# Mixture of eight experts on one core: the x of experts 0 and 1 as two halves of one tile

## The chip, the cores and the metric

The kernel runs on 1 core of one Trainium2 chip. The metric is device time in microseconds (us) of one execution; the time of a kernel is the median of several executions. A core has five engines that run side by side: TensorE (PE; its weight loads are shown as PEld), VectorE (DVE), ScalarE (ACT), GpSimd (POOL) and SyncE (SP). Transfers between the chip's main memory (HBM) and the core's memory (SBUF, 128 partitions) run on 16 DMA engines. POOL, SP and ACT can issue transfers, each into a queue of its own: in the profile q0 holds what POOL issues, q1 what SP issues, q10 what ACT issues.

## The reference

Each of 8 experts has 256 tokens of 512 numbers and two layers; all inputs are fp32.

```python
n_experts, capacity, hidden, expert_hidden = 8, 256, 512, 2048
# x [8,256,512]  w1 [8,512,2048]  w2 [8,2048,512]  b1 [8,2048]  b2 [8,512]
h = np.matmul(x, w1) + b1[:, np.newaxis, :]
h = np.maximum(h, 0)
return (np.matmul(h, w2) + b2[:, np.newaxis, :]).astype(np.float32)
```

One expert has 4.2 MB of w1 and as much of w2, so the weights are 67 MB in all; x and the result are 4.2 MB each.

## The kernel before, in words

All products are made in fp16 with fp32 sums. POOL's transfers turn fp32 in HBM into fp16 in SBUF on the way; SP's and ACT's move bytes as they are.

*Staging.* `w1_sb[e]` is a tile of 128 partitions, each with 4 rows of w1 (16 KB in fp16), `w2_sb[e]` one with 16 rows of w2 for each partition. Both come from pools of three buffers, so the load for expert e waits until the products of expert e-3 have read that buffer. The loads stand in `ring` (lines 260 to 270), an order with a stage for each: within a stage x (where `X_LOADS` has it), then w1, then w2 of the expert three behind. POOL issues them in that order (`ordered` keeps a queue's instructions in the order of the program).

*x and its turning.* The first product needs x with its 512 numbers along the partitions, so x has to be turned. There are three ways:
- Experts 4 to 7: one load by POOL (`load_x`, line 80), turned by DVE in 32x32 blocks (`turn_on_vector`, line 118).
- Experts 2 and 3: one load by POOL into one tile. Each expert has 64 partitions, each with R = 4 tokens. PE turns both experts together (`turn_on_tensor(2, 2)`, line 103): for two of the four rows at a time, 8 transposes of 128x128 into the PSUM tile `pt`, of which there is one buffer, and one copy on DVE (line 114, an "eviction") into `turned`. The columns of a turned block are then 64 tokens of one expert and 64 of the other, so an expert's x is 4 runs of 64 columns.
- Experts 0 and 1: SP loads each as fp32 into a tile of its own, with 128 partitions of R = 2 tokens, 4 KB (lines 224 to 227). DVE casts each to fp16 (line 247), and PE turns each by itself with `turn_on_tensor(e, 1)`: 8 transposes, one eviction.

PE's transposes need the unit matrix `ident`, which POOL, DVE and ACT make at the start (lines 236 to 243). DVE's order at the start is: `steps_turned` (line 240), then for each of experts 0 and 1 the cast and the eviction, then four transposes that lay out b1 as `b1T` (line 253), which wait for b1's own small load, `b_rows`.

*The products.* `first_product(e)` has 16 groups of 4 matmuls into a PSUM tile `ph` (three buffers); after each group ACT adds b1, applies the relu and writes `hT` (`relu`, line 130). The relu puts the tokens in the order that the store wants, by two forms of its access pattern that depend on R = `x16[e][2]`. Three stages later `second_product(e)` adds b2 and multiplies with w2 into `po`, and `store` copies `po` to an fp32 tile in SBUF.

*Results.* Experts 0 to 3 share one result tile (tag `out0`), experts 4 and 5 another (tag `out4`, 128 partitions of 8 KB, `group_pool`); POOL stores both at the end (`flush`). Experts 6 and 7 each have a tile of the pool `out_pool`, tag `out`, with two buffers, and are stored by SP and ACT. The two fp32 tiles for the x of experts 0 and 1 are the first two users of those buffers.

*The order of products* is the loop at line 272: in stage s the first product of expert s, then the second product of expert s-3.

Of the kernel before, what the change touches and what calls it, by code (L numbers as in the profile page):

```python
# [10 lines left out]
def kernel(  # L11
# [9 lines left out]
    nc = tc.nc  # L21
    fp32 = mybir.dt.float32
    fp16 = mybir.dt.float16
    E, T, H = x.shape
    M = w1.shape[2]
    P = 128
    nTB = T // P
# [8 lines left out]
    GROUPS = {0: 4, 4: 2}  # L36
# [5 lines left out]
    nXF32 = 2  # L42
# [3 lines left out]
    def ordered(ins):  # L46
        return tc.keep_in_program_order(ins)
# [4 lines left out]
    x_pool = ctx.enter_context(tc.tile_pool(name="xp", bufs=1))  # L52
# [3 lines left out]
    group_pool = ctx.enter_context(tc.tile_pool(name="groups", bufs=1))  # L56
    out_pool = ctx.enter_context(tc.tile_pool(name="outp", bufs=2))
# [13 lines left out]
    x16 = [None] * E  # L71
# [18 lines left out]
    def load_w1(e):  # L90
        w1_sb[e] = w1_pool.tile([P, nKC, M], fp16, tag="w1", name="w1sb")
        ordered(nc.gpsimd.dma_start(  # L92
            out=w1_sb[e], in_=w1[e].rearrange("(p kc) m -> p kc m", kc=nKC)
        ))
# [8 lines left out]
    def turn_on_tensor(first, n):  # L103

        t, _, R = x16[first]
        turned = turned_pool.tile([P, nKC, R, P], fp16, tag=f"turned{first}", name=f"turned{first}")
        for lo in range(0, R, nTB):
            pt = psum_x.tile([P, nKC, nTB, P], fp16, tag="pt", name="pt")
            for r in range(nTB):
                rows = t[:, lo + r, :].rearrange("p (i kc) -> p kc i", kc=nKC)  # L110
                for kc in range(nKC):
                    ordered(nc.tensor.transpose(  # L112
                        out=pt[:, kc, r, :], in_=rows[:, kc, :], identity=ident))
            ordered(nc.vector.tensor_copy(out=turned[:, :, lo : lo + nTB, :], in_=pt))  # L114
        for i in range(n):
            xT[first + i] = turned[:, :, :, i * (P // n) : (i + 1) * (P // n)]
# [104 lines left out]
                    ))  # L221
        store(e, po)

    x32 = []
    for e in range(nXF32):
        x32.append(out_pool.tile([P, nTB, H], fp32, tag="out", name="x32"))
        nc.sync.dma_start(out=x32[e], in_=x[e].rearrange("(p tb) h -> p tb h", tb=nTB))
    load_w1(0)
    ordered(nc.gpsimd.dma_start(  # L229
        out=b2_sb,  # L230
        in_=b2.rearrange("e h -> (e h)").rearrange("(o f) -> o f", o=1),
# [9 lines left out]
    for b in range(nB):  # L241
        part = slice(b * B, (b + 1) * B)
        nc.scalar.copy(out=ident[part, part], in_=steps_turned[part, :, 0])  # L243

    for e in range(nXF32):
        t = x_pool.tile([P, nTB, H], fp16, tag=f"x{e}", name=f"x{e}")
        ordered(nc.vector.tensor_copy(out=t, in_=x32[e]))  # L247
        x16[e] = (t, 0, nTB)
        turn_on_tensor(e, 1)


    for b in range(nB):
        ordered(nc.vector.transpose(  # L253
            out=b1T[b * B : (b + 1) * B, nB - 1 - b : nB - 1 - b + nJ * B],
            in_=b1_rows.rearrange("r (i j) -> r j i", j=nJ),
# [55 lines left out]
```

## Time and profile before

| | us |
|---|---|
| median of 3 executions | 181.64 |
| lowest and highest | 181.51, 182.15 |
| the profiled execution, its own time | 181.3 |
| its span in the trace | 179.5 |
| PE busy with matmuls | 133.4 |
| DVE busy | 42.9 |
| ACT busy | 72.6 |
| POOL busy | 14.9 |

The span is the time from the first to the last event of the core in the trace; the 1.8 us between it and the execution's time lie around it. Times inside the trace are counted from the start of the span. In the page's list of the span in 40 slices each digit is the busy share of a slice, in tenths. In a group of instructions, "x8" is how many there were, "128x1024 f16<-128x1024 f32" the shape and type of what is written and read, and what stands behind "<-" in brackets or behind a bar is the idle time of the engine just before and what ended it. The trace moved 40.55 MB of written bytes through the DMA engines, and read 71.39 MB of HBM.

### The profile page before, as it was taken

To read this page: it belongs to the slowest core of one execution; us is meant where nothing else is said; L and a number is where in the kernel's file an instruction comes from. 1 tells how busy PE (TensorE), PEld (TensorE's weight loads), DVE (VectorE), ACT (ScalarE), POOL (GpSimd) and SP (SyncE) were. 2 spreads that over 40 slices of the span, in tenths; PEclk is the share of its full clock that TensorE was granted. 3 is DMA by queue.
4 is the path that set the end of the run, shared out by engine and by line. 5 is a ranking of instruction groups with operands and counts; after the bars stand their busy time and mean duration, and the time that the engine had idled before them with its cause. 6 is when DMAs were issued, how large, how long until landed. Compare 5 with 4: busy or idle time off the path is not lost.

```text
span 179.5 us, 1952 instructions
## 1 busy us (share of the span) xinstructions
PE 133.4 (74%) x816; PEld 89.7 (50%) x816; DVE 42.9 (24%) x47; ACT 72.6 (40%) x157; POOL 14.9 (8%) x33
## 2 busy tenths in 40 slices
PE   0226499969499930999869994959798899999660
PEld 0114389969387410793358543933387343343220
DVE  0615400020000199409700691000600030301010
ACT  2200379939367250491167406940298002011010
POOL 7300003010201010001100001000100002002000
PEclk9999999999979996599987999987999699999998
DMA  5999999998998999999899999989999999999995
GB/s 207 260 223 203 234 204 204 234 230 179 236 230 184 228 234 208 201 234 226 190 226 234 204 204 234 223 186 234 226 194 223 234 204 203 212 218 219 329 434 248
DMA packets 3827, 40.55 MB, mean 226 GB/s; under 512 B 460, under 2 KB 476, under 8 KB 1260
## 3 DMA queue, kind: packets, MB, share of 16 engines
q0 software_dynamic: 3232, 38.35, 96.5%
q1 hardware_dynamic: 476, 1.70, 2.5%
q10 hardware_dynamic: 112, 0.39, 0.6%
q8 instruction: 6, 0.10, 0.2%
q14 instruction: 1, 0.01, 0.0%
HBM read 71.39 MB, written 4.19 MB: 421 GB/s over the span
## 4 chain that ended last, share of the span: by engine, by line
DMA 55%; PE 33%; another core or an unknown queue 3%; POOL 3%; ACT 2%; issue 1%; POOLq 0%
DMA w1sb<-in_w_dram 44%; PE ph L158 16%; PE po L215 16%; DMA w2sb<-in_w_dram 11%; ACT out L194 2%; PE po L208 1%; POOL w1sb L92 1%; POOL steps L236 1%; POOL x L84 0%; POOL w2sb L101 0%; POOL b_sb L229 0%; POOL b_rows L233 0%; ACT hT L145 0%; POOL steps L237 0%
## 5 line engine op out<-in xcount | busy, mean ns | idle before, releaser
L158 PEld LDWEIGHTS <-w1sb 128*128 128x128 f16 x512 | 60.6, 148 | 31.8 <-DMA w1sb<-in_w_dram 25.0
L145 ACT ACTIVATE hT<-ph,b1T 128x256 f16<-128x256 f32 x128 | 56.4, 474 | 33.3 <-PE ph L158 19.7
L215 PE MATMUL po<-w2sb,hT 128*128 128x512 f16 x256 | 59.9, 394 | 6.0 <-DMA w2sb<-in_w_dram 6.0
L215 PEld LDWEIGHTS <-hT 128*128 128x128 f16 x256 | 25.7, 101 | 40.1 <-issue 13.8
L158 PE MATMUL ph<-xT,w1sb 128*128 128x256 f16 x256 | 32.5, 293 | 14.1 <-DMA w1sb<-in_w_dram 13.9
L158 PE MATMUL ph<-turned,w1sb 128*128 128x256 f16 x256 | 33.7, 300 | 10.9 <-DMA w1sb<-in_w_dram 8.5
L194 ACT COPY out<-po 32x512 f32<-32x512 f32 (+2 forms) x22 | 12.7, 579 | 59.8 <-PE po L215 59.7
L124 DVE STREAM_TRANSPOSE xT<-x 32x1024 f16<-32x1024 f16 x16 | 19.8, 1236 | 43.5 <-DMA x<-in_x_dram 24.5
L193 DVE COPY out<-po 32x512 f32<-32x512 f32 (+2 forms) x20 | 13.8, 689 | 57.2 <-PE po L215 56.9
L101 POOL DMA_DIRECT2D w2sb<-in_w_dram x10 | 5.3, 534 | 72.3 <-PE po L215 72.3
L92 POOL DMA_DIRECT2D w1sb<-in_w_dram x8 | 4.8, 594 | 63.8 <-PE ph L158 63.0
L112 PE MATMUL pt<-ident,x 128*128 128x128 f16 x32 | 3.3, 263 | 8.8 <-ACT ident L243 6.7
L114 DVE COPY turned<-pt 128x1024 f16<-128x1024 f16 x4 | 2.8, 692 | 19.5 <-PE pt L112 19.5
L112 PEld LDWEIGHTS <-x 128*128 128x128 f16 x32 | 2.6, 126 | 9.2 <-DVE x L247 8.3
L253 DVE STREAM_TRANSPOSE b1T<-b_rows 32x512 f32<-32x512 f32 x4 | 4.1, 1034 | 4.8 <-DMA b_rows<-in_b_dram 4.8
L208 PE MATMUL po<-b_sb,ones 1*128 1x512 f16 x16 | 4.8, 379 | 0.0
L193 ACT COPY out<-po 32x512 f32<-32x512 f32 x2 | 1.2, 576 | 3.9 <-PE po L215 3.9
L243 ACT COPY ident<-steps_turned 32x32 f16<-32x32 f16 x4 | 1.0, 242 | 3.5 <-DVE steps_turned L240 3.5
L240 DVE STREAM_TRANSPOSE steps_turned<-steps 128x1024 f16<-128x1024 f16 x1 | 1.2, 1246 | 4.2 <-POOL steps L237 4.2
L208 PEld LDWEIGHTS <-ones 1*128 1x128 f16 x16 | 0.9, 92 | 2.1 <-issue 2.1
L243 ACT ACT_TABLE_LOAD x1 | 1.3, 1283 | 0.7 <-PEq L295 0.7
L247 DVE CAST x<-x 128x1024 f16<-128x1024 f32 x2 | 1.3, 667 | 0.0
(13 smaller groups left out, 5.5 us busy)
## 6 DMA issues: line engine op xcount, KB each, us to landing
w1sb<-in_w_dram POOLq DMA_DIRECT2D x8, 2048.0 KB, 34.5
w2sb<-in_w_dram POOLq DMA_DIRECT2D x6, 2048.0 KB, 48.2
w2sb<-in_w_dram POOLq DMA_DIRECT2D x2, 1024.0 KB, 27.2
out_dram<-out POOLq DMA_DIRECT2D x1, 2048.0 KB, 12.7
w2sb<-in_w_dram POOLq DMA_DIRECT2D x1, 1152.0 KB, 19.8
x<-in_x_dram SPq DMA_DIRECT2D x2, 512.0 KB, 3.7
x<-in_x_dram POOLq DMA_DIRECT2D x1, 1024.0 KB, 32.6
out_dram<-out POOLq DMA_DIRECT2D x1, 1024.0 KB, 8.3
```

The lines of the kernel that those rows point to most:

```text
L92: ordered(nc.gpsimd.dma_start(out=w1_sb[e], in_=w1[e].rearrange("(p kc) m -> p kc m", kc=nKC)))
L101: ordered(nc.gpsimd.dma_start(out=w2_sb[e][:, lo:hi], in_=src[:, lo:hi]))
L112: ordered(nc.tensor.transpose(out=pt[:, kc, r, :], in_=rows[:, kc, :], identity=ident))
L114: ordered(nc.vector.tensor_copy(out=turned[:, :, lo : lo + nTB, :], in_=pt))
L124: nc.vector.transpose(out=turned[b * B : (b + 1) * B], in_=src.rearrange("p r (i kc) -> p kc r i", kc=nKC),)
L145: nc.scalar.activation(out=out, in_=columns, func=mybir.ActivationFunctionType.Relu, bias=b1T[:, bias_at : bias_at + 1], scale=1.0,)
L158: ordered(nc.tensor.matmul(out=ph, lhsT=w1_sb[e][:, kc, :].rearrange("p (q j) -> p q j", j=nJ)[:, :, j], rhs=xT[e][:, kc], start=(kc == 0) ...
L193: on(out=out_sb[at : at + rows, k, :], in_=po[0][part])
L194: nc.scalar.copy(out=out_sb[at : at + rows, split + k, :], in_=po[1][part])
L208: ordered(nc.tensor.matmul(out=t, lhsT=ones1, rhs=b2_sb[0:1, e * H : (e + 1) * H], start=True, stop=False,))
L215: ordered(nc.tensor.matmul(out=po[tb], lhsT=hT[e][:, j, tb * P : (tb + 1) * P], rhs=w2_sb[e][:, j, :], start=False, stop=(j == nJ - 1),))
L253: ordered(nc.vector.transpose(out=b1T[b * B : (b + 1) * B, nB - 1 - b : nB - 1 - b + nJ * B], in_=b1_rows.rearrange("r (i j) -> r j i", j=nJ),
```

## The change

The fp32 x of experts 0 and 1 goes into one tile of 128 partitions with 4 tokens each (8 KB). Expert 0 has partitions 0 to 63, expert 1 partitions 64 to 127. SP still issues two loads of 512 KB, each as 64 rows of 8 KB into its half. DVE casts each half by itself, 64 partitions of 2,048 numbers. PE then turns both together with `turn_on_tensor(0, 2)`, as for experts 2 and 3. Since R is now 4 for these two experts, their first products read 4 runs of 64 columns and their relu uses the access pattern of experts 2 and 3. The number of transposes (16), of evictions (2) and of all other instructions is the same. The fp32 tile takes the room of the result tile of experts 4 and 5 (tag `out4`), and the buffers of `out_pool` belong to experts 6 and 7 alone.

The order on the engines: DVE has both casts, then both evictions, where it had cast, eviction, cast, eviction. PE's 16 transposes all read the common tile. POOL's order is the same.

```diff
-    x32 = []
+    R0 = nXF32 * T // P
+    x32 = group_pool.tile([P, R0, H], fp32, tag=f"out{max(GROUPS)}", name="x32")
+    of_expert = [slice(e * (P // nXF32), (e + 1) * (P // nXF32)) for e in range(nXF32)]
     for e in range(nXF32):
-        x32.append(out_pool.tile([P, nTB, H], fp32, tag="out", name="x32"))
-        nc.sync.dma_start(out=x32[e], in_=x[e].rearrange("(p tb) h -> p tb h", tb=nTB))
+        nc.sync.dma_start(out=x32[of_expert[e]], in_=x[e].rearrange("(p r) h -> p r h", r=R0))
     load_w1(0)
...
+    t = x_pool.tile([P, R0, H], fp16, tag="x0", name="x0")
     for e in range(nXF32):
-        t = x_pool.tile([P, nTB, H], fp16, tag=f"x{e}", name=f"x{e}")
-        ordered(nc.vector.tensor_copy(out=t, in_=x32[e]))
-        x16[e] = (t, 0, nTB)
-        turn_on_tensor(e, 1)
+        ordered(nc.vector.tensor_copy(out=t[of_expert[e]], in_=x32[of_expert[e]]))
+        x16[e] = (t, e * (P // nXF32), R0)
+    turn_on_tensor(0, nXF32)
```

## The prediction

> **What bounds the kernel now.** I read the page first: the slices over time, then the queues, then the chain that ended last.
>
> ```profile
> span 179.5 us, 1952 instructions
> ...
> PE 133.4 (74%) x816; PEld 89.7 (50%) x816; DVE 42.9 (24%) x47; ACT 72.6 (40%) x157; POOL 14.9 (8%) x33
> ...
> DMA  5999999998998999999899999989999999999995
> ...
> q0 software_dynamic: 3232, 38.35, 96.5%
> q1 hardware_dynamic: 476, 1.70, 2.5%
> ...
> DMA 55%; PE 33%; another core or an unknown queue 3%; POOL 3%; ACT 2%; issue 1%; POOLq 0%
> ```
>
> From the second slice to the last but one the DMA engines are full, while PE is busy 74% of the span. Queue q0 alone, which carries all the weights, takes 96.5% of the time of 16 engines. The busy times in stages say the same; the columns used here are the stretch and, at the end of each row, the DMA share and the GB/s.
>
> ```profile
> core 0: us, PE busy (x) PEld busy (x) DVE busy (x) ACT busy (x) POOL busy (x), PEclk, DMA share, GB/s
> 1.80:2.50 0.70, 0.00 (x0) 0.00 (x0) 0.00 (x0) 0.23 (x1) 0.70 (x3) 1.00 0.75 181
> 2.50:4.50 2.00, 0.00 (x0) 0.00 (x0) 0.26 (x1) 0.00 (x0) 2.00 (x6) 1.00 0.98 401
> ...
> 5.40:14.60 9.20, 2.06 (x16) 1.55 (x16) 2.65 (x5) 0.97 (x4) 0.78 (x1) 1.00 0.95 203
> 30.00:120.00 90.00, 70.92 (x489) 53.78 (x488) 28.03 (x28) 49.39 (x108) 4.97 (x10) 0.92 1.01 216
> ...
> 168.00:178.00 10.00, 4.04 (x18) 1.66 (x17) 0.69 (x1) 0.59 (x1) 0.00 (x0) 1.00 0.97 404
> ```
>
> The share is about 1.0 in every stage. Written bytes run at 216 GB/s where fp32 weights become fp16 on the way, and at 401 to 404 where fp32 stays fp32 (x at the start, the results at the end). So the kernel is one stream of transfers. The chain in order of time shows how far that stream's issues run ahead:
>
> ```profile
> 5.33 32.66 DMA w1sb<-in_w_dram
> ...
> 149.49 19.77 DMA w2sb<-in_w_dram
> ```
>
> w1 of expert 2 is issued by 5.33 and lands at 38.0; the last w2 piece is issued by 149.5 and lands at 169.3. The engines always have a backlog of ten microseconds or more. What makes the stream itself longer therefore moves the end one for one; what makes a compute engine later moves it only beyond the backlog.
>
> **The change part by part.**
>
> *The two loads of x.* Still two SP issues of 512 KB; each now fills 64 partitions with 8 KB, in place of 128 partitions with 4 KB. The DMA view of three stretches shows when x (q1) moves, and that w1 (q0) follows it.
>
> ```profile
> q1 hardware_dynamic: 34, 0.14, 26.2%
> ...
> q1 hardware_dynamic: 212, 0.80, 98.4%
> ...
> q1 hardware_dynamic: 288, 1.05, 53.5%
> q0 software_dynamic: 16, 0.26, 23.4%
> ```
>
> The first row is 0 to 2.5 us, the second 2.5 to 4.5, the last two 0 to 5.4. After a start of 0.14 MB, x fills the engines alone (98.4% in the second row); of w1 only 16 packets, one for each engine, begin before 5.4. While x moves, all 128 partitions together take 401 GB/s, 3.1 GB/s each. The end of the kernel, 404 GB/s, is no faster. No stretch in which the engines are full shows a partition at more than about that. The changed loads give the same engines half as many partitions at a time; to keep pace each would have to take 6.3 GB/s.
>
> No row shows a saturated load to 64 partitions, so I bound it. Below: nothing but packet size, half as many packets for the same bytes. Even if x moved at the best 426 GB/s that a half-microsecond of the load shows,
>
> ```profile
> 4.00:4.50 0.50, 1.00 1.03 426
> ```
>
> the remaining 1.05 - 0.14 = 0.91 MB would take 2.14 us for 0.91/0.401 = 2.27, a gain of 0.13. Above: a partition takes no more than now, the rate halves to 200 GB/s, and 0.91 MB takes 4.54 us, a loss of 2.27; with the start slowed alike it is 1.05/0.401 = 2.62. Between them lies 216 GB/s, the rate of writing while the weights stream, which gives 0.91/0.216 = 4.21, a loss of 1.94. I take +2.1, the middle of 1.94 and 2.27, because both rows of fp32 traffic (401 and 404) sit at the same rate per partition, and keep -0.13 and +2.62 as ends.
>
> The Trainium skill, SBUF — State Buffer, section "Door 1: The DMA port swizzle", speaks against the change: 64 adjacent partitions reach 8 of 16 ports, and it gives 196 GB/s for 1 MiB to partitions 0 to 63 against 328 to all 128; its section "Can I just issue two DMAs to hit both halves?" gives only 6% more for a pair at partitions 0 and 64. An estimate from that page is 1.05/0.208 - 1.05/0.328 = 1.85 us more; this trace holds no run that tests it.
>
> *The casts and the turning by PE.* The work around x as it stands:
>
> ```profile
> 4.24 1.25 DVE L240 STREAM_TRANSPOSE steps_turned<-steps 128x1024 f16<-128x1024 f16 x1 [4.24 <-POOL steps L237]
> ...
> 5.33 0.86 POOL L92 DMA_DIRECT2D w1sb<-in_w_dram  x1
> 5.41 0.65 DVE L247 CAST x<-x 128x1024 f16<-128x1024 f32 x1
> ...
> 6.67 1.01 PE L112 MATMUL pt<-ident,x 128*128 128x128 f16 x8 [6.67 <-ACT ident L243]
> 7.72 0.69 DVE L114 COPY turned<-pt 128x1024 f16<-128x1024 f16 x1 [1.66 <-PE pt L112]
> 8.33 0.68 DVE L247 CAST x<-x 128x1024 f16<-128x1024 f32 x1
> ...
> 9.07 1.04 PE L112 MATMUL pt<-ident,x 128*128 128x128 f16 x8 [1.38 <-DVE x L247]
> 10.15 0.69 DVE L114 COPY turned<-pt 128x1024 f16<-128x1024 f16 x1 [1.14 <-PE pt L112]
> ...
> 15.26 2.79 PE L158 MATMUL ph<-turned,w1sb 128*128 128x256 f16 x12 [5.15 <-DMA w1sb<-in_w_dram]
> 15.63 4.17 DVE L253 STREAM_TRANSPOSE b1T<-b_rows 32x512 f32<-32x512 f32 x4 [4.79 <-DMA b_rows<-in_b_dram]
> ...
> 28.61 0.53 POOL L92 DMA_DIRECT2D w1sb<-in_w_dram  x1 [22.43 <-PE ph L158]
> ```
>
> Each cast now has half the partitions and twice the columns: 0.67 us (unchanged) if its time goes by elements, 1.33 if by columns. The groups of copies of 512 columns on the same engine decide:
>
> ```profile
> L193 DVE COPY out<-po 32x512 f32<-32x512 f32 x14 | 9.6, 688 | 17.7 <-PE po L215 17.5
> ...
> L193 DVE COPY out<-po 128x512 f32<-128x512 f32 x2 | 1.4, 692 | 16.1 <-PE po L215 16.1
> ```
>
> 32 and 128 partitions take 688 and 692 ns, so I take 1.33, and two casts cost 2.67 for 1.33. Both casts now come before the first transpose, since a 128x128 block holds rows of both experts. Still 16 transposes and two evictions of 1,024 columns, with one PSUM buffer between them. The two loads of x, issued at 0.75 and 1.16, now land 3.4 and 4.1 us later:
>
> ```profile
> L227 SPq DMA_DIRECT2D x<-in_x_dram x2: 400/408/416, 0.7 to 1.2; - x2
> ...
> DMA to landing us min/median/max: 3.4/3.7/4.1
> ```
>
> With the second landing at 5.3 + 2.1 = 7.4: first cast 5.4 to 6.7, second 7.4 to 8.7, transposes to 9.8, eviction to 10.5, transposes to 11.6, eviction to 12.3. Now the end is 10.84. The 1.5 us cost nothing while the first w1 lands later: 15.25 now, 17.3 then. Even if that cover went, the first product on expert 0 frees w1's buffer for the issue at 28.61, and what was issued before it lasts to 38.0: 9.4 us of lateness is free. Behind the longer casts on DVE only the b1T transposes wait, which start at 15.63 for their own load.
>
> The POOL issue at 5.33 took 0.86 us, beside a median of 0.53, and lies beside a cast:
>
> ```profile
> L92 POOL DMA_DIRECT2D w1sb<-in_w_dram x8: 530/532/857, 1.3 to 81.3; - x8
> ```
>
> A longer cast may stretch it by another 0.67; the transfer lands at 38.0 and, at 2.1 MB and 216 GB/s, takes 9.7 us, so it begins near 28, and I cost the issue at nothing.
>
> *The first products and the relu.* Experts 0 and 1 now read their turned x as 4 runs of 64 columns, as experts 2 and 3 do already, and their relu reorders as for those.
>
> ```profile
> L158 PE MATMUL ph<-turned,w1sb x256: 272/273/441, 15.3 to 56.3; 128*128 128x256 f16 x128
> ...
> L145 ACT ACTIVATE hT<-ph,b1T x128: 467/474/476, 19.9 to 138.0; 128x256 f16<-128x256 f32 x128
> ```
>
> The first row holds both forms and its least and median differ by 1 ns; the relu of all experts lies within 9 ns. Nothing. The fp32 tile takes its room from the results of experts 4 and 5, which are first written long after the casts:
>
> ```profile
> 145.26 1.39 DVE L193 COPY out<-po 64x512 f32<-64x512 f32 x2 [16.73 <-PE po L215]
> ```
>
> Nothing. Second products and stores are untouched.
>
> Sum: +2.1 of transfer and 0 of the rest. The profiled execution took 181.3 us, its span of 179.5 and 1.8 around it; the median 181.64 is 0.34 above. The forecast is 181.64 + 2.1 = 183.7 us.
>
> **Rivals.** *The half costs nothing.* The engines, not the partitions, set the 401 GB/s. For it: the shares are 1.0 in all stages, and reading fp32 at 2 x 216 = 432 GB/s fits a limit of the engines. It decides if x of expert 1 still lands by 5.3. Time 181.6, or 181.5 with the packets' gain: not slower.
>
> *w1 fills the gaps.* w1's packets enter as soon as its descriptors exist and use what x leaves idle. Then only x of expert 0 pays: its 0.52 - 0.14 = 0.38 MB takes 1.90 for 0.95 us, +0.95, 182.6. Against it: the rows above show one w1 packet for each engine, and those only at x's end. The Trainium skill, DMA: Bandwidth & Descriptors, section "Queues, rings and completion order", says that an engine goes round its queues at packet granularity, which would favour this; what the trace shows up to 5.4 us can't tell it from w1 not being ready.
>
> *Late x uncovers PE.* If w1 instead pushes x of expert 1 back behind several of its packets, the first product starts after w1's landing. Since 9.4 us of lateness are free it must reach beyond 28 us for its ready time; one more microsecond then gives 184.7. Nothing speaks for it.
>
> **How the numbers follow.** Forecast 0.64, nothing lost 0.21, gaps filled 0.08, late x 0.02, none of these 0.05. A change of 0.5% (0.9 us) is about what can be told from none. The filled gaps, at +0.95, lie on that bound and are split. Slower: 0.64 + 0.04 + 0.02 = 0.70. Same: 0.21 + 0.04 = 0.25. Faster: the unnamed 0.05, since no row offers over 0.13. The forecast's own range is +1.9 to +2.62 about, 183.5 to 184.3. The range reaches to the case of no loss and its run-to-run spread below, 181.4, and to +2.62 with the 0.34 between two executions above, 184.6.
>
> **What the changed profile would show.** Right: x's two loads fill q1 until about 7 us at near 200 GB/s, x's second landing over 6 us after its issue for 4.1 now; first w1 matmul near 17.3; everything after it, the last w2 landing too, 2 us later; DMA share 1.0. Casts of 1.3 us, PE waiting for w1 and not for x. Wrong: q1 done by 5 us, or w1's first matmul at 15.3, or a later first matmul with the last landing still at 169.3, which would mean that the stream had slack that I don't see.

## The result and the profile after

| | before | after |
|---|---|---|
| median of 13 executions, us | 181.62 | 182.18 |
| lowest and highest | 181.31, 182.15 | 181.88, 183.13 |
| the profiled execution | 181.3 | 182.08 |
| its span | 179.5 | 180.3 |

The ratio after to before is 1.0033, 95% interval 1.0019 to 1.0046: slower, by 0.3 to 0.8 us. The direction is the one forecast, the size (+2.1 us) is not, and 182.18 lies within what the prediction called no change, under 0.5%.

The page of the changed kernel, the lines that answer to those of before:

```profile
span 180.3 us, 1950 instructions
...
DMA  7999999899999989998999999899999999999995
...
q0 software_dynamic: 3232, 38.35, 96.0%
q1 hardware_dynamic: 348, 1.70, 2.9%
```

The stream is as full as it was. q1 has 128 packets fewer and yet a larger share, 2.9% for 2.5%. The stages of the changed kernel, with the DMA share and GB/s at the end of each row:

```profile
1.80:2.50 0.70, 0.00 (x0) 0.00 (x0) 0.00 (x0) 0.23 (x1) 0.70 (x3) 1.00 0.98 187
2.50:4.50 2.00, 0.00 (x0) 0.00 (x0) 0.26 (x1) 0.00 (x0) 2.00 (x6) 1.00 1.36 320
...
5.40:14.60 9.20, 1.04 (x8) 0.88 (x9) 2.55 (x4) 0.96 (x4) 1.38 (x1) 1.00 1.08 256
30.00:120.00 90.00, 71.06 (x483) 52.53 (x482) 28.02 (x28) 48.43 (x106) 4.78 (x9) 0.92 1.02 218
```

The later stages are those of before; the start differs. How it does is seen in the queues: the DMA view of the changed kernel for 3.1 to 3.9 us, for 5 to 9, and for 0 to 12 (packets, MB, share of 16 engines).

```profile
q1 hardware_dynamic: 32, 0.26, 152.6%
...
q0 software_dynamic: 41, 0.67, 78.5%
q1 hardware_dynamic: 48, 0.39, 24.1%
...
q0 software_dynamic: 96, 1.57, 61.3%
q1 hardware_dynamic: 160, 1.05, 29.6%
```

A packet counts in whole in the stretch in which it starts, so a share can pass 100%. A share times the stretch times 16, over the packets, is the mean time of a packet. In 3.1 to 3.9, the later half of the first load of x, it is 1.526 x 0.8 x 16 / 32 = 0.61 us for 8 KB. In 5 to 9, the second load, it is 0.241 x 4 x 16 / 48 = 0.32. And in that stretch w1 moves 0.67 MB beside x's 0.39. The second load is not slow, and it is not alone: its packets take turns with w1's, and it needs until 12 us.

The work around x, from the timeline of the changed kernel:

```profile
0.74 1.18 SPq L228 DMA_DIRECT2D x<-in_x_dram  x2
...
5.32 1.47 POOL L92 DMA_DIRECT2D w1sb<-in_w_dram  x1
5.44 1.22 DVE L248 CAST x<-x 64x2048 f16<-64x2048 f32 x1
...
12.18 1.23 DVE L248 CAST x<-x 64x2048 f16<-64x2048 f32 x1 [5.52 <-DMA x<-in_x_dram]
...
17.05 4.19 DVE L254 STREAM_TRANSPOSE b1T<-b_rows 32x512 f32<-32x512 f32 x4
17.07 2.72 PE L158 MATMUL ph<-turned,w1sb 128*128 128x256 f16 x12 [0.78 <-DVE turned L114]
...
28.00 0.53 POOL L92 DMA_DIRECT2D w1sb<-in_w_dram  x1 [21.22 <-PE ph L158]
```

The second cast waits 5.5 us for x; the first product begins at 17.07 for 15.26, now held by x's turning and no longer by w1. That it begins close to the 17.3 of the forecast is luck, since the forecast had it wait for w1. The lateness costs nothing: the issue which waits for this product comes at 28.00, and came at 28.61 before.

One instruction serves as a mark of how late the stream is: POOL's copy of one number (line 174), which waits for the landing of the last w2's first piece. Before, and then after:

```profile
163.62 0.18 POOL L174 COPY landed<-w2sb 1x1 f16<-1x1 f16 x1 [13.59 <-DMA w2sb<-in_w_dram]
```

```profile
164.36 0.18 POOL L174 COPY landed<-w2sb 1x1 f16<-1x1 f16 x1 [15.35 <-DMA w2sb<-in_w_dram]
```

The mark is 0.74 us later. w1 of expert 2, the first DMA piece of the chain after, is as late already:

```profile
5.32 33.42 DMA w1sb<-in_w_dram
```

5.32 + 33.42 = 38.74 for 5.33 + 32.66 = 37.99 before, 0.75 later. So the whole loss is there by 38.7 us, and the stream carries it to the end unchanged. The two profiled executions are 182.08 - 181.3 = 0.8 us apart, a little more than the medians (0.56), so a mark, which is read from one execution, is good to some 0.2 us.

### The profile page after: what moved, and what is told of

It is laid out like the page before. It is cut to its first block, busy times and chain, and to the rows that moved or that the text cites. A ratio compares the mean times of both kernels' runs of the same rounds, so it can differ in the third digit from the quotient of the medians.

```text
span 180.3 us, 1950 instructions
## 1 busy us (share of the span) xinstructions
PE 130.0 (72%) x816; PEld 87.5 (49%) x816; DVE 44.1 (24%) x47; ACT 72.1 (40%) x157; POOL 15.4 (9%) x33
## 4 chain that ended last, share of the span: by engine, by line
DMA 66%; PE 26%; POOL 2%; another core or an unknown queue 1%; issue 1%; ACT 0%; POOLq 0%
DMA w1sb<-in_w_dram 44%; DMA w2sb<-in_w_dram 22%; PE po L215 17%; PE ph L158 8%; PE po L208 1%; POOL w1sb L92 1%; POOL steps L237 1%; ACT out L194 0%; POOL x L84 0%; POOL b_sb L230 0%; POOL b_rows L234 0%; POOL steps L238 0%; POOL ident L239 0%; POOL ones L240 0%
## 5 line engine op out<-in xcount | busy, mean ns | idle before, releaser
L158 PEld LDWEIGHTS <-w1sb 128*128 128x128 f16 x512 | 58.1, 146 | 24.2 <-DMA w1sb<-in_w_dram 18.7
L215 PE MATMUL po<-w2sb,hT 128*128 128x512 f16 x256 | 61.2, 401 | 9.3 <-DMA w2sb<-in_w_dram 9.3
L158 PE MATMUL ph<-xT,w1sb 128*128 128x256 f16 x256 | 31.7, 288 | 12.0 <-DMA w1sb<-in_w_dram 11.6
L158 PE MATMUL ph<-turned,w1sb 128*128 128x256 f16 x256 | 30.0, 280 | 7.6 <-DMA w1sb<-in_w_dram 4.7
L92 POOL DMA_DIRECT2D w1sb<-in_w_dram x8 | 5.4, 670 | 61.6 <-PE ph L158 60.8
L248 DVE CAST x<-x 64x2048 f16<-64x2048 f32 x2 | 2.4, 1222 | 5.5 <-DMA x<-in_x_dram 5.5
```

Source lines behind the costliest of these rows:

```text
L92: ordered(nc.gpsimd.dma_start(out=w1_sb[e], in_=w1[e].rearrange("(p kc) m -> p kc m", kc=nKC)))
L158: ordered(nc.tensor.matmul(out=ph, lhsT=w1_sb[e][:, kc, :].rearrange("p (q j) -> p q j", j=nJ)[:, :, j], rhs=xT[e][:, kc], start=(kc == 0) ...
L215: ordered(nc.tensor.matmul(out=po[tb], lhsT=hT[e][:, j, tb * P : (tb + 1) * P], rhs=w2_sb[e][:, j, :], start=False, stop=(j == nJ - 1),))
```

## The experiments

Theories. (1) The forecast's: one partition takes no more than about 3.1 GB/s, and 64 at a time halve the rate. (2) Neighbouring partitions share ways into the memory, and the lower half has half of the ways. (3) The loss is from the larger packets, SP's longer issues or the order of casts and transposes. A second question is why only a quarter of the forecast loss came.

### One load in place of two

```diff
-    for e in range(nXF32):
-        nc.sync.dma_start(out=x32[of_expert[e]], in_=x[e].rearrange("(p r) h -> p r h", r=R0))
+    nc.sync.dma_start(out=x32, in_=x[0:nXF32].rearrange("e (p r) h -> (e p) r h", r=R0))
```

> The two loads of x become one: 128 partitions with 8 KB each, one SP issue of 1 MB; casts, turning and all else as in the changed kernel. If the loss comes from filling half the partitions at a time, each 8 KB packet takes about 0.31 us as the first ones of the changed kernel did, x is in by about 5 us, w1 follows it as before the change, and the time is back at 181.6 (181.4 to 181.8). If it comes from the larger packets or from the casts standing ahead of the transposes, it stays at 182.2. The second cast then starts by 7 us and not at 12.2.

Measured: 181.57 us, ratio to before 1.0001 (0.9987 to 1.0015). Its DMA view from 2.7 to 4.5 us:

```profile
q1 hardware_dynamic: 89, 0.73, 95.7%
```

0.957 x 1.8 x 16 / 89 = 0.31 us a packet. Packets of 8 KB, casts by halves and the common turning cost nothing that shows (0.15% at most). Its mark is at 163.81, 0.19 later than before. The loss is in the two loads: in the partitions that they fill, or in their being two.

### Every other partition

```diff
-        nc.sync.dma_start(out=x32[of_expert[e]], in_=x[e].rearrange("(p r) h -> p r h", r=R0))
+        nc.sync.dma_start(out=x32[e :: nXF32], in_=x[e].rearrange("(p r) h -> p r h", r=R0))
```

> Still two SP loads of 64 rows of 8 KB, but each into every other partition of the tile (expert 0 in the even ones, expert 1 in the odd ones). The tokens of the two experts are then mixed in the products, so the results of experts 0 and 1 are not the reference's; work and sizes are the same. If a single partition takes no more than about 3.1 GB/s (the mechanism of the forecast), 64 partitions are still too few: packets of about 0.62 us in the first load, time 182.2. If it is neighbouring partitions that share a way into the memory, so that the lower half has only half of the ways, both loads run at 0.31 us a packet, x is in by about 5.3 us, and the time is 181.6 to 181.9 (0.28 us for the longer issues on SP may stay).

Measured: 181.92 us, ratio 1.0023 (1.0009 to 1.0036). The DMA view from 2.7 to 3.5 us, the first load:

```profile
q1 hardware_dynamic: 36, 0.29, 94.2%
```

0.942 x 0.8 x 16 / 36 = 0.33 us a packet, with 64 partitions. Theory (1) falls. Yet the time does not go back all the way. SP's two issues of 64 rows take 1.17 us (1.18 in the changed kernel) for 0.87 before, and x's second load takes turns with w1 here as well, where it was expected to be in by 5.3 us. The second cast is as late as in the changed kernel and the first product later still:

```profile
12.68 2.46 DVE L248 CAST x<-x 64x2048 f16<-64x2048 f32 x2 [7.20 <-DMA x<-in_x_dram]
18.81 2.72 PE L158 MATMUL ph<-turned,w1sb 128*128 128x256 f16 x12 [0.78 <-DVE turned L114]
```

The first product is 3.5 us later than before, with a mark at 164.03, only 0.41 later: the lateness of PE does not reach the stream.

### The loads by themselves

> No products: loads of x alone, one after another, each waiting for the one before, and a copy of one tile as the result (not the reference's). 512 KB each into: all 128 partitions; 0 to 63; 64 to 127; 32 to 95; every other one; 0 to 31 with 16 KB each; then 0 to 63 and 64 to 127 issued together; then 1 MB to all 128. All twice. If a partition's own rate is the limit: 1.25 us of transfer for all 128, 2.5 for every set of 64 (32 to 95 and every other one too), 5 for 0 to 31. If neighbours share ways and the lower and the upper half have half of them each: 1.25 for all 128, 2.5 for 0 to 63 and 64 to 127 and about 2.5 for 0 to 31, but 1.25 for 32 to 95 and for every other one; the pair together about 5, the 1 MB 2.5.

The edit is a new kernel body: a list of such loads on SP, each behind a 1x1 copy on DVE that waits for the load before. It ran once.

```diff
+    t = room(f"mid_{i}", 4)
+    after_the_last(t, 32)
+    load(t[32:96], rows(3, 64))
```

The stretches of seven loads of the second round, from the first packet to the last, with GB/s at the end: 0 to 63; 64 to 127; 32 to 95; every other; 0 to 31; the pair; 1 MB to all 128.

```profile
43.45:46.09 2.64, 1.00 0.79 196
48.23:50.88 2.65, 1.00 0.84 198
53.23:55.17 1.94, 1.00 0.85 270
57.00:58.83 1.83, 1.00 0.79 282
60.34:62.94 2.60, 1.00 0.84 202
65.33:70.17 4.84, 1.00 0.96 217
72.28:75.77 3.49, 1.00 0.87 300
```

In the first round the same seven took 2.50, 2.40, 1.94, 2.08, 2.76, 4.88 and 3.41 us, so a stretch repeats to within some 0.25. The 512 KB to all 128 partitions took 2.01 and 2.02 in the two rounds, no less than 32 to 95.

The order of theory (2) holds in both rounds. 64 neighbouring partitions are slow if they are one half, and not slow if they lie across the middle. 32 partitions that take 16 KB each (2.76 and 2.60) are about as fast as 64 that take 8 (2.50 and 2.64), where theory (1) has them take twice as long. The Trainium skill, SBUF — State Buffer, section "Door 1: The DMA port swizzle", has this map: by its table partitions 0 to 63, like 0 to 31 and 64 to 127, reach 8 of 16 ports. It gives 196 GB/s for 1 MiB to partitions 0 to 63; 512 KB from its first packet to its last moved at 196 here in the second round and, in 2.50 us, at 210 in the first.

The sizes differ from what was expected. A load of one half takes 0.46 to 0.71 us more than one across the middle and not twice as long, and the pair takes 4.88 and 4.84 for 3.41 and 3.49 in one load, 1.47 and 1.35 more.

### w1 issued later, in the changed kernel and in the one before

The same edit in both, named e3 in the changed kernel and e5 in the one before:

```diff
+    ordered(nc.gpsimd.memset(steps, 0.0))
+    ordered(nc.gpsimd.memset(steps.rearrange("p n c -> p (n c)")[:, :: B + 1], 1.0))
+    ordered(nc.gpsimd.memset(ident, 0.0))
+    ordered(nc.gpsimd.memset(ones1, 1.0))
     load_w1(0)
...
-    nc.gpsimd.memset(steps, 0.0)
-    nc.gpsimd.memset(steps.rearrange("p n c -> p (n c)")[:, :: B + 1], 1.0)
-    nc.gpsimd.memset(ident, 0.0)
-    nc.gpsimd.memset(ones1, 1.0)
```

> The changed kernel with POOL's four memsets ahead of the first w1 issue, which moves that issue by some 1.6 us (1.25 to about 2.9). If w1's packets between those of the second x load are what hid its slowness, the second load now runs alone from 4.3 us on with packets of about 0.62 us until w1 begins near 5.9, so q1 moves at about 200 GB/s there; time 182.7 to 183.2. If the second load is not slow at all, its packets stay at 0.32 us, it is done by 5.7, and the engines stand idle until w1 begins.

> The kernel before with POOL's four memsets ahead of the first w1 issue, as the control of the changed kernel with the same edit. x is in by 5 us as in the kernel before; w1 begins when it is ready, some 1.6 us later than it was ready before. If w1 is ready near 3.6 us without the edit, it begins near 5.2 to 5.9 and the engines idle for 0.3 to 1 us: 181.8 to 182.6, some 0.8 to 1.5 below the changed kernel with this edit (183.35). If it is the same as that one, the edit itself and not the slow second load cost the time there.

Measured: 183.35 us in the changed kernel, ratio 1.0101 (1.0068 to 1.0134); 181.83 in the one before, 1.0019 (1.0009 to 1.0030). The issue moved by 0.9 us, from 1.25 to 2.17, less than expected. The DMA views of both for 0 to 5.4 us, e3 first:

```profile
q1 hardware_dynamic: 112, 0.79, 62.2%
```

```profile
q1 hardware_dynamic: 288, 1.05, 54.4%
q0 software_dynamic: 15, 0.25, 22.2%
```

In the kernel before, x is in and w1 has begun on 15 engines by 5.4 us, as without the edit, so the edit leaves no gap there; it costs 0.2 to 0.5 us all the same, and the cause of that is open. In the changed kernel w1 has not begun, and 0.26 MB of x are missing. From 3.1 to 6.6 us only x moves:

```profile
q1 hardware_dynamic: 112, 0.79, 107.0%
```

Of these 112 packets 96 carry data (0.79 MB / 8 KB): 1.07 x 3.5 x 16 / 96 = 0.62 us each, in both loads. So the second load is slow when it runs alone, and it is w1's packets in between that hide it. What the change costs then is the difference of the two kernels with the edit, by the medians 183.35 - 181.83 = 1.5 us, beside the 1.35 and 1.47 of the pair by itself, where the changed kernel without the edit lost 0.56. The marks, e3 first, are 1.88 us apart:

```profile
165.73 0.18 POOL L174 COPY landed<-w2sb 1x1 f16<-1x1 f16 x1 [15.28 <-DMA w2sb<-in_w_dram]
```

```profile
163.85 0.18 POOL L174 COPY landed<-w2sb 1x1 f16<-1x1 f16 x1 [15.29 <-DMA w2sb<-in_w_dram]
```

The profiled execution of e5 was its fastest, so 1.88 may be high; the intervals of the two ratios leave room for 0.7 to 2.3 us.

### A loss twice as large

The kernel with one load of x, and a further 1 MB ahead of it, which nothing reads. The twin has `extra[32:96]`.

```diff
+    extra = group_pool.tile([P, 2 * R0, H], fp32, tag="out0", name="extra")
+    ordered(nc.sync.dma_start(
+        out=extra[0:64], in_=x[2:4].rearrange("e (p r) h -> (e p) r h", r=2 * R0)))
```

> The kernel with one load of x (128 partitions), and ahead of it on SP one more load of 1 MB that nothing reads, as 64 rows of 16 KB into partitions 0 to 63. Theory now: partitions 0 to 63 have half of the ways into the memory, and time that the engines lose there before w1 begins is lost to the end. The extra load then takes 1.05 MB / 205 GB/s = 5.1 us, against some 2.5 to 3 with all ways: 2 us or more over the twin with partitions 32 to 95, and about 186.5 to 187 in all. Rival: what the first load loses is given back later in the stream (the stream has slack); then the twins are equal to 0.3 us.

> The same with the extra 1 MB as 64 rows of 16 KB in partitions 32 to 95. Theory now: full rate, 1.05 MB at about 400 GB/s, so 181.6 + 2.6 = 184.2 (183.9 to 184.7), 2 us or more below its twin. Rival (the rate of single partitions, or of 64 partitions whichever they are): as slow as its twin.

Measured: 187.02 us with the lower half, ratio 1.0301 (1.0286 to 1.0316), and 184.86 across the middle, 1.0204 (1.0171 to 1.0237; its executions spread from 184.43 to 186.64). The mark, lower half first:

```profile
168.63 0.18 POOL L174 COPY landed<-w2sb 1x1 f16<-1x1 f16 x1 [15.28 <-DMA w2sb<-in_w_dram]
```

```profile
166.77 0.18 POOL L174 COPY landed<-w2sb 1x1 f16<-1x1 f16 x1 [15.28 <-DMA w2sb<-in_w_dram]
```

Both came out above what was expected, 187.02 for 187 at most and 184.86 for 184.7. The twins differ in the 64 partitions alone, and by 1.86 us at the mark, 2.2 by the medians. A loss at the start is not given back.

### One load and one cast

```diff
-    for e in range(nXF32):
-        ordered(nc.vector.tensor_copy(out=t[of_expert[e]], in_=x32[of_expert[e]]))
+    ordered(nc.vector.tensor_copy(out=t, in_=x32))
+    for e in range(nXF32):
```

It has the single load as well.

> One load of x into 128 partitions and one cast of 128 x 2048 in place of two of 64 x 2048. One cast of 1.22 us where two took 2.45; PE's turning ends 1.2 us earlier. Both theories: w1 lands later than that in either case, so the time stays at 181.6 (181.4 to 181.8), the same as the kernel with one load and two casts.

Measured: 182.00 us, ratio 1.0032 (1.0021 to 1.0043), a miss. PE's turning does end earlier, and the mark is where it is with two casts: 163.82 for 163.81. The spans are 179.8 and 179.9. What differs lies outside the span: 182.06 - 179.8 = 2.26 us in the profiled execution, and 181.75 - 179.9 = 1.85 with two casts. All seven executions have 2.14 to 2.26 us outside the span. The two kernels ran on different chips, but that is not the reason: the twins above and e5 ran on the same chip as this one and have 1.73 to 1.86. Nothing in the trace explains it; it stays open. No kernel tried beats the one before.

## Why the prediction was right or wrong

*The stream as the bound: right.* The loss of the start stands at the mark near 164 unchanged: 0.75 us at 38.7 and 0.74 there in the changed kernel.

*The rate of the loads: right in that it can halve, wrong in why.* The later packets of the first load take 0.61 us, where those of the single load take 0.31. But the limit that I drew from 3.1 GB/s for each partition does not exist: 32 partitions took 202 GB/s, 6.3 each. It is the choice of partitions, as the Trainium skill, SBUF — State Buffer, section "Door 1: The DMA port swizzle", says of the two halves; no row of before could show it. My words beside the forecast, "64 adjacent partitions", say too much: 32 to 95 are adjacent too and were not slow.

*The size: the step that failed.* The sum let all 0.91 MB after the start run at the slow rate, for +2.1 us; the medians moved by 0.56. Two things are in its place.
- The second load did not run alone. The forecast read the one w1 packet for each engine, at x's end, as if w1 could not come in earlier. In the changed kernel it comes in as soon as the first load is in, and the second load's packets, which take turns with it, take 0.32 us and not 0.61. So only the first load was slow. This was the rival "w1 fills the gaps", to which I gave 0.08 and 182.6 us. Its mechanism is shown by e3, where w1's absence makes the second load slow and the kernel 1.2 us slower than the changed one (of which the edit itself costs 0.2 to 0.5 in the kernel before). Its price of +0.95 was too high as well.
- A slow load is not slow from its first packet on. The packets that the engines start between 2.8 and 3.1 us, the second of the first load's four on each, took 0.32 us as in a fast load (16 packets with a share of 105.0%: 1.05 x 0.3 x 16 / 16). Only the two after them took twice as long, 0.3 us more each, which fits the 0.46 to 0.71 that a load of one half costs by itself. Why the first packets escape is open. Whether the pair alone in the kernel would have cost the 2.1 is not settled: 1.35 and 1.47 by themselves, 1.5 by the medians of e3 and e5, 1.9 by their marks. The estimate of 1.85 beside the forecast let the pair run alone as well.

*What is left of the 0.56.* By the marks, the late start and the taking of turns cost 164.03 - 163.81 = 0.22 (every other partition against one load), the slow half 164.36 - 164.03 = 0.33. By the ratios it is the other way round: 0.23% (0.42 us) stays with every other partition, 0.1 us of it outside the span, and only 0.10% (0.18 us) goes. The marks rest on single profiled executions, and the intervals of the ratios (1.0009 to 1.0036 and 1.0019 to 1.0046) overlap, so the split is not settled. The longer issue on SP was in no term of my sum: I counted the two issues as unchanged.

*The casts: right.* 1.22 us each for 1.33 forecast. *The POOL issue beside the cast* took 1.47 for 0.86, +0.61 where up to 0.67 was allowed, at no cost that shows. *The first products and the relu: right*, as the least and median show:

```profile
L158 PE MATMUL ph<-turned,w1sb x256: 270/273/418, 17.1 to 55.4; 128*128 128x256 f16 x128
...
L145 ACT ACTIVATE hT<-ph,b1T x128: 467/475/478, 21.3 to 138.2; 128x256 f16<-128x256 f32 x128
```

*Late x: the mechanism of this rival came, to which I gave 0.02 since nothing spoke for it; its price did not.* w1 pushed x's second load back to a landing at 12 us, not 7.4, and PE waited for x where I had said for w1. The free lateness is borne out as far as it was tried: 1.8 us in the changed kernel and 3.5 with every other partition, of the 9.4 that I read, did not reach the stream.

## What to carry to other kernels

Where the transfers are the bound, ask of each load which partitions it fills: 64 in one half of the memory took 2.40 to 2.65 us for 512 KB, 64 across the middle 1.94. Then ask what else the engines can do meanwhile: the packets of the same load took 0.62 us each when it ran alone and 0.32 when another queue's packets took turns with them. Two loads of the two halves are better issued as one load of all 128 partitions, which here brought back the time of before.

## What the runs showed that I had not expected

An SP issue of 64 rows took 0.47 to 0.60 us and one of 32 or 128 rows 0.33 to 0.38 in the kernel of loads alone, although it makes no more packets than 128 rows do. Rows alone do not decide it: behind the further 1 MB of the last twins, the issue of 128 rows took 0.57 and 0.58. The first packet followed the longer issue later too: by the start of the stream, 2.07 us in the changed kernel for 1.79.

Whether SP's second load and w1 take turns goes along with when their issues end. SP's second issue and POOL's of w1 end together, within 0.05 us, in the changed kernel (both 1.92 us), with every other partition and in the twins with a further 1 MB: there w1 takes turns with the second load. SP's ends earlier in the kernel before (1.62 for 1.92), in e5 (1.63 for 2.84) and in e3 (1.92 for 2.84): there the second load runs to its end ahead of w1. In the changed kernel:

```profile
0.74 1.18 SPq L228 DMA_DIRECT2D x<-in_x_dram  x2
1.25 0.67 POOL L92 DMA_DIRECT2D w1sb<-in_w_dram  x1 [0.80 <-POOLq L296]
```

How long the first load takes does not explain it. With every other partition the first load is fast, and w1 comes in all the same: by 3.9 us 16 of its packets have begun, where the kernel before, with the same POOL issue, has none. e3 moves w1's issue against the changed kernel, and the turns are gone; no run moves SP's issue alone, so the order is what the runs have in common and not a shown cause.
